# A two-layer encoder trunk on one core: two projection stages written out in program order with GpSimd reduced to one operation, and the attention buffers laid out anew around the last output weights

## The chip, the cores and the metric

The kernel runs on one core of one Trainium2 chip. The metric is the time of one execution in device microseconds (us), the median of several runs. A core has TensorE (PE; its weight loads are listed as PEld), VectorE (DVE), ScalarE (ACT), GpSimd (POOL) and SyncE (SP). DMAs are issued from SP and from ACT here, and both queues run on the same 16 DMA engines.

## The reference

Two layers of three parallel head groups over 1024 positions of width 1024, everything in float32:

```python
def hybrid_layer(x, g_norm, w_in, ...):
    h = rms_norm(x, g_norm)
    z = jnp.einsum('bsd,dc->bsc', h, w_in)             # 1024 -> 2656 columns
    aq, ak, av, ag, bq, bk, bv, bg, cq, ckv, ckr, cg = jnp.split(z, idx, axis=-1)
    qa, ka = (apply_axial_rope(rms_norm(t, g), ...) for t, g in ((aq, a_qn), (ak, a_kn)))
    oa = dense_gqa_blocks(qa, ka, va, HEAD_DIM ** -0.5) * jax.nn.silu(ag)      # A: 6 heads, 2 kv
    qb, kb = (apply_rope(t, ...) for t in (bq, bk))
    ob = windowed_sink_gqa(qb, kb, vb, b_sink, HEAD_DIM ** -0.5) * jax.nn.silu(bg)  # B: |i-j| <= 128
    qc = einsum(rms_norm(cq, c_qn), c_wuq); kv = einsum(rms_norm(ckv, c_kvn), c_wukv)
    oc = mla_blocks(qc_nope, rope(qc_rope), kc_nope, rope(ckr), vc, 96 ** -0.5) * jax.nn.silu(cg)  # C: 4 heads
    return x + jnp.einsum('bsm,md->bsd', concatenate([oa, ob, oc]), w_out)
```

A last RMSNorm closes the trunk.

## The kernel before

**Numbers.** Every float32 operand of a matmul is split into a rounded part (hi, the letter h at a tile's end) and a rest (lo, l); a product is three matmuls (`mm3`, L119). hi is a copy or cast on ACT or POOL, lo a subtraction on DVE that follows it.

**Stages of a layer.** The 1024 positions are 8 row tiles of 128 (`st`). (1) The rows are normalised, transposed to `hTh`/`hTl`, and the v columns of A and B are projected (`v_rows`). (2) **Stage A**, a loop over `st`: 24 matmuls of 512 columns give the q and k columns (`pza`), ACT copies them (`za`) and squares them (`ta`), DVE sums the squares (`ssa`, `ms_a`), POOL raises to the power -1/2 (`rs_a`, L113), DVE scales, and the axial rotation is a product with the cosines (`ta`, POOL L364), four products with the sines (`ua`, DVE L372) and a sum (DVE L377). `qk_out` transposes a finished row on PE (`pqka`, L301), splits it and stores it; `flush(2)` calls it two rows later. (3) **Stage B**, the same without the norm; its cosine product is POOL L397. In rows of A the weights of B are loaded and split step by step (`w_steps`: hi on POOL L196, lo on DVE L197), in rows of B those of C's projection. (4) C's latent projections, and the gates (`pg`, SiLU on ACT, stored by ACT's queue to `d_gate`). (5) **Attention**: `units` lists score units. For each `qt` (128 queries) and each of two kv heads there are three units of A and one of B; the scores are `sa`, `sb`, `sc`, the transposed probabilities `ppa`.. and the values `poa`... Behind the units of `2 * qt + kv` in `C_AT` comes a list of C's units. (6) **Output projection**: `out_part(st, c, ...)` sums 8 products with `Wo` into a bank of PSUM (`pw`), in two column halves c; the first `MW` = 5 of the 8 Wo tiles are used as spare work in the attention's end (`load_wo(wa_.wa, m)`), the last 3 come from a pool `wb` opened after it. DVE adds the residual (`y`, L1155), and the next layer's norm is mixed in.

**What sets the order.** A Tile scheduler reorders each engine's instructions by a simulated timeline, and pools decide which tiles share memory: a tile that lies over an older one waits for its last reader. SP issues its DMAs in one order; each carries one of eight semaphores (DMAHW0 to 7), taken in turn by the DMAs of SP and ACT, and waits there for the DMA that had it before.

**Memory in the attention.** The pools `at`, `ck` (k1, k2, k3 and the values `vC` of C), `qg` (C's queries `qc` and the gates gta, gtb, gtc) are stacked; `wb` opens over their upper part, on vC, qc and the gates. Stage (6) has three banks of PSUM for `pw` (`ps_s`); a fourth bank, `ps_o`, belongs to the value products.

Of the kernel before, what the change touches and what calls it, by code (L numbers as in the profile page):

```python
# [32 lines left out]
C_AT = (1, 3, 4, 6, 8, 9, 11, 13)  # L33
WARM = 12
PV_PRIO = 0
# [9 lines left out]
def kernel(  # L45
# [54 lines left out]

    ident = const.tile([P, P], F32, name="ident")
# [22 lines left out]
    class Stage:  # L124
# [17 lines left out]
        def norm(self, st, xt, src, junk):  # L142

            ss = small.tile([P, 1], F32, tag="ss1", name=f"ss{self.l}_{st}")
            nc.scalar.activation(junk, src, AF.Square, accum_out=ss)
            r = rstd_of(ss, D, f"x{self.l}_{st}", 1)
            nc.vector.scalar_tensor_tensor(xt, src, r[:, 0:1], self.ng, ALU.mult, ALU.mult)

        def turn(self, st, xt, ps_t):
            hf, c0 = st // 4, (st % 4) * P  # L150
            for g in range(2):
                pt = ps_t(f"pt{self.l}_{st}_{g}")
                for j in range(4):
                    nc.tensor.transpose(
# [14 lines left out]
        def w_steps(self, ws, pieces, eng=nc.vector, pool=None):  # L169
# [4 lines left out]
            for k0 in range(0, ND, kt):  # L174
# [31 lines left out]
    for l in range(DEPTH):  # L206
# [18 lines left out]
        with stage.ph as ph:  # L225
# [26 lines left out]
            def v_rows(st):  # L252
                ps = gemm_sc(stage.wv, st, f"pzv{l}_{st}")
                pv_ = ps[:, 0:256].rearrange("p (h d) -> p h d", d=64)
                nc.scalar.copy(vAB[:, st, :, 0:64], pv_)
                nc.vector.tensor_sub(vAB[:, st, :, 64:128], pv_, vAB[:, st, :, 0:64].bitcast(F32))

            if l == 0:
                stage.open_px()
                warm = ps_o("warm")  # L260
                for _ in range(WARM):
                    nc.tensor.matmul(warm[:, 0:P], lhsT=ident, rhs=ident, start=True, stop=True)
                xts = []
                for st in range(NS):
                    xts.append(stage.px.tile([P, D], F32, tag="xt", name=f"xt{l}_{st}", bufs=NS))
                    queue_behind[0] = dma(xts[st], x_src[st * P : (st + 1) * P, :])
                    if st == 0:
                        dma(stage.ng, norm_g[l].partition_broadcast(P))
                        stage.load_wv()
                for st, xt in enumerate(xts):  # L270
# [19 lines left out]
            dma(rope_b, c_rope_b.rearrange("(n p) t d -> p n t d", p=P))  # L290
            dma(rope_c, c_rope_c.rearrange("(n p) t d -> p n t d", p=P))
# [3 lines left out]
            def qk_out(u, g, st, nk):  # L295

                nm = f"{g}{l}_{st}"
                n = 3 + nk
                pt = ps_t(f"pqk{nm}")
                for j in range(n):  # L300
                    nc.tensor.transpose(pt[:, j * P : (j + 1) * P], u[:, j * P : (j + 1) * P], ident)  # L301
# [3 lines left out]
                nc.scalar.copy(hi[:, 0:n, :], ptv)  # L305
                nc.vector.tensor_sub(lo[:, 0:n, :], ptv, hi[:, 0:n, :].bitcast(F32))
# [945 lines left out]
```

## Time and profile before

| | |
|---|---|
| runs | 1353.19, 1356.27, 1358.64 us; median 1356.27 |
| the profiled execution | 1353.11 us, its span 1351.3 us, mean granted TensorE clock 0.993 |
| busy share of the span | PE 97%, PEld 84%, DVE 66%, ACT 52%, POOL 44% |
| DMA | 166.46 MB, mean 123 GB/s |

All times of a stage are counted in us from the span's start. In layer 0, stage A's matmuls begin at 44.2 and those of C's projection at 144.6, the gates end at 282.8, the attention runs to 588.8 and the output projection follows; the other layer repeats it some 670 us later. A PE busy share of 97% hides where its idle time lies, so a stage is read by windows and by waits.

### The profile page before, as it was taken

The page shows a single profiled execution, that of the slowest core. Times are in us where ns is not written, and L with a number is a line of the kernel's source. Part 1 is how long each engine was busy: PE and PEld are TensorE (multiplying, and loading weights), DVE is VectorE, ACT ScalarE, POOL GpSimd, SP SyncE. Part 2 cuts the span into 40 slices and gives each one's busy share as a digit, 9 for nine tenths or more (in the row PEclk, how much of TensorE's full clock was granted, in tenths as well). Part 3 has the DMA queues.
Part 4 walks back from the last instruction along what each step waited for, and adds up shares of the span by engine and source line. Part 5 has one row for each costly group of instructions (what it writes and reads, how often), then busy time and mean ns, then how long its engine had stood idle before and what let it go on. Part 6 is the DMA issues. An engine that isn't in the chain of part 4 may idle for free.

```text
span 1351.3 us, 21770 instructions
## 1 busy us (share of the span) xinstructions
PE 1307.1 (97%) x7320; PEld 1135.8 (84%) x7320; DVE 898.1 (66%) x2198; ACT 697.9 (52%) x1503; POOL 598.0 (44%) x694
## 2 busy tenths in 40 slices
PE   7999999999999999989999999999999999999897
PEld 7877998879998998867898779888799989988686
DVE  7586762058888889855436766610798889888533
ACT  5121341168888888712222214411788889887222
POOL 2564221026766766741025621200377676678200
PEclk9999999999999999999999999999999999999999
DMA  7333469443222511456323425694422225114443
GB/s 238 117 109 117 142 209 259 136 133 100 61 71 68 140 46 45 134 166 194 110 81 100 131 94 161 214 251 117 144 79 63 71 68 140 46 32 154 136 140 114
DMA packets 176879, 166.46 MB, mean 123 GB/s; under 512 B 22528, under 2 KB 149376, under 8 KB 176768
## 3 DMA queue, kind: packets, MB, share of 16 engines
q1 hardware_dynamic: 158016, 140.43, 35.6%
q10 hardware_dynamic: 18752, 24.65, 5.4%
q8 instruction: 58, 0.95, 0.3%
q14 instruction: 53, 0.43, 0.1%
HBM read 107.35 MB, written 57.67 MB: 122 GB/s over the span
## 4 chain that ended last, share of the span: by engine, by line
PE 64%; DVE 10%; ACT 6%; DMA 6%; POOL 5%; issue 4%; SPq 1%; POOLq 0%; DVEq 0%; ACTq 0%
PE pg L119 13%; PE pw L119 8%; PE poa L119 6%; PE ppa L655 5%; PE sa L119 4%; PE sc L119 4%; PE pzc L119 4%; PE pzb L119 4%; PE poc L119 3%; PE ppc L655 3%; DMA wst<-in_w_in_dram 2%; DVE ua L372 2%; PE pob L119 2%; PE sb L119 2%; POOL rs_a L113 2%
## 5 line engine op out<-in xcount | busy, mean ns | idle before, releaser
L636 DVE CUSTOM_DVE_ANT_0 pa<-sa,zero 128x512 f32<-128x512 f32 x96 | 65.6, 683 | 140.8 <-PE sa L119 135.1
L664 POOL TENSOR_TENSOR ptla<-pfa,ptha 128x512 fp32r<-128x512 f32 x96 | 123.9, 1293 | 5.8
L663 POOL TENSOR_SCALAR ptha<-pfa 128x512 fp32r<-128x512 f32 x96 | 59.7, 624 | 145.0 <-ACT pfa L662 136.7
L119 PE MATMUL sa<-ka,qsta 128*128 128x512 f32 x384 | 120.7, 417 | 0.7 <-ACT g L571 0.7
L646 ACT ACTIVATE pa<-pa,nmxa 128x1024 f32<-128x1024 f32 x96 | 111.3, 1161 | 17.7 <-DVE nmxa L636 15.6
L119 PE MATMUL pw<-woh,oh 128*128 128x512 f32 x256 | 101.1, 403 | 13.6 <-POOL woh L969 9.1
L119 PE MATMUL sc<-k,qc 128*128 128x512 f32 x384 | 109.9, 408 | 0.0
L655 PE MATMUL ppa<-ident,pa 128*128 128x128 f32 x768 | 107.3, 273 | 0.2
L655 PEld LDWEIGHTS ppa<-ident,pa 128*128 128x128 f32 x768 | 91.0, 141 | 14.2 <-DVE ptla L667 1.7
L119 PE MATMUL pw<-wol,oh 128*128 128x512 f32 x256 | 102.0, 400 | 0.4
L119 PE MATMUL pg<-hTh,wh 128*128 128x512 f32 x256 | 100.3, 392 | 0.0
L119 PE MATMUL pw<-woh,ol 128*128 128x512 f32 x256 | 99.9, 398 | 0.2 <-DVE ol L954 0.2
L119 PE MATMUL pg<-hTh,wl 128*128 128x512 f32 x256 | 100.1, 391 | 0.0
L119 PE MATMUL pg<-hTl,wh 128*128 128x512 f32 x256 | 100.0, 391 | 0.0
L196 POOL TENSOR_SCALAR wh<-wst 128x512 fp32r<-128x512 f32 (+2 forms) x96 | 59.2, 635 | 83.3 <-DMA wst<-in_w_in_dram 48.4
L119 PE MATMUL poa<-ptha,vAB 128*128 128x384 f32 x256 | 88.6, 346 | 0.9 <-ACT pc L646 0.5
L571 ACT ACTIVATE g<-pg 128x512 f32<-128x512 f32 x32 | 19.2, 599 | 134.8 <-PE pg L119 99.4
L119 PE MATMUL poa<-ptla,vAB 128*128 128x384 f32 x256 | 87.6, 342 | 0.0
L197 DVE TENSOR_TENSOR wl<-wst,wh 128x512 fp32r<-128x512 f32 (+2 forms) x96 | 67.5, 733 | 27.2 <-POOL wh L196 27.2
L646 ACT ACTIVATE pc<-pc,nmxc 128x1024 f32<-128x1024 f32 x64 | 74.2, 1161 | 10.0 <-DVE nmxc L636 9.5
L664 POOL TENSOR_TENSOR ptlc<-pfc,pthc 128x512 fp32r<-128x512 f32 x56 | 75.7, 1360 | 1.2
L119 PEld LDWEIGHTS sc<-k,qc 128*128 128x128 f32 x384 | 66.7, 189 | 9.9 <-DVE nmxc L636 0.9
(210 smaller groups left out, 3855.0 us busy)
## 6 DMA issues: line engine op xcount, KB each, us to landing
wst<-in_w_in_dram SPq DMA_DIRECT2D x20, 512.0 KB, 3.8
d_gate<-g ACTq DMA_DIRECT2D x32, 256.0 KB, 3.1
wost<-in_w_out_dram SPq DMA_DIRECT2D x32, 256.0 KB, 2.8
wst<-in_w_in_dram SPq DMA_DIRECT2D x16, 384.0 KB, 4.0
qsta<-d_qa SPq DMA_DIRECT2D x64, 96.0 KB, 2.8
qstb<-d_qb SPq DMA_DIRECT2D x64, 96.0 KB, 2.6
k<-d_kn SPq DMA_DIRECT2D x12, 512.0 KB, 5.8
qc<-d_qc SPq DMA_DIRECT2D x96, 64.0 KB, 2.2
```

Source lines behind the costliest of these rows:

```text
L113: last_pow[0] = nc.gpsimd.tensor_tensor(out=r, in0=ms, in1=mhalf[:, 0:w], op=ALU.pow).ins
L119: nc.tensor.matmul(ps, lhsT=a, rhs=b, start=first and i == 0, stop=last and i == len(parts) - 1)
L196: nc.gpsimd.tensor_scalar(h, f, 1.0, 0.0, ALU.mult, ALU.add)
L197: eng.tensor_tensor(out=r, in0=f, in1=h.bitcast(F32), op=ALU.subtract)
L372: nc.vector.tensor_mul(u5[:, h0:h1, :, a, :], z5[:, h0:h1, :, 1 - a, :], s5[:, :, a, :].unsqueeze(1).to_broadcast([P, nh, 2, 16]),)
L571: nc.scalar.activation(g, ps, AF.Silu)
L636: nc.vector.tensor_tensor_reduce(p[:, c * 512 : (c + 1) * 512], ps, zero[:, 0:1].to_broadcast([P, 512]), -1.0, nmx[0][:, 0:1] if c else 3. ...
L646: nc.scalar.activation(p, p, AF.Exp, scale=-1.0, bias=nmx[1][:, 0:1], accum_out=sm)
L655: nc.tensor.transpose(pt[:, (j - q0) * P : (j - q0 + 1) * P], p[:, j * P : (j + 1) * P], ident)
L663: nc.gpsimd.tensor_scalar(hi, f, 1.0, 0.0, ALU.mult, ALU.add)
L664: nc.gpsimd.tensor_tensor(out=lo, in0=f, in1=hi.bitcast(F32), op=ALU.subtract)
```

## The change

1. **Program order in A and B.** The engines are wrapped; while `pinned[0]` is set, an instruction keeps its place in program order. The two loops are written as a pipeline: a row's matmuls, the transposes of the row two before, ACT's square ahead of its copy, DVE's sums, POOL's power, the last sum of the row before (`add_halves`), the split of the transposed row (`qk_split`), one weight step, then the scaling and the products.
2. **GpSimd.** In A and B it keeps only the power; the cosine products go to DVE, the hi casts of B's and C's weights to ACT.
3. **Loads.** A's weights are asked for ahead of the tables, two rope tables after them; x has 6 buffers instead of 8.
4. **Pools of the attention.** New order `at`, `cv` (vC), `qg` (gates), `ck` (k1, k2, k3), `qc` (C's queries); `wb` opens over C's keys and queries.
5. **Output projection.** hi of the last three Wo tiles is made by ACT; one bank in four of `pw` is `ps_o`, and a fourth partial sum, (1, 1), joins the spare work.
6. **`C_AT`** starts (2, 3, 5, 6, ...) instead of (1, 3, 4, 6, ...).

```diff
-C_AT = (1, 3, 4, 6, 8, 9, 11, 13)
+C_AT = (2, 3, 5, 6, 8, 9, 11, 13)
+XBUFS = 6
+    pinned = [False]
+    class Engine:
+        def __init__(self, eng):
+            self.eng = eng
+        def __getattr__(self, op):
+            f = getattr(self.eng, op)
+            if not pinned[0]:
+                return f
+            return lambda *a, **k: tc.keep_in_program_order(f(*a, **k))
+    V, G, A, T = Engine(nc.vector), Engine(nc.gpsimd), Engine(nc.scalar), Engine(nc.tensor)
...
-                    nc.gpsimd.tensor_scalar(h, f, 1.0, 0.0, ALU.mult, ALU.add)
-                    eng.tensor_tensor(out=r, in0=f, in1=h.bitcast(F32), op=ALU.subtract)
+                    if hi_eng is A:
+                        A.copy(h, f)
+                    else:
+                        G.tensor_scalar(h, f, 1.0, 0.0, ALU.mult, ALU.add)
+                    V.tensor_tensor(out=r, in0=f, in1=h.bitcast(F32), op=ALU.subtract)
...
+            def add_halves():
+                for u, t in halves:
+                    V.tensor_add(u, t, u)
+                halves.clear()
+            pinned[0] = True
+            pb = pb_.enter_context(tc.tile_pool(name=f"pb{l}", bufs=1, reuse_waits="tile"))
+            ws_b = [], [], 512
+            steps = stage.w_steps(ws_b, [(1024, 512)], A, pb)
             for st in range(NS):
                 ps = gemm_sc(ws, st, f"pza{nm}")
-                flush(2)
+                old = late.pop(0) if len(late) > 1 else None
+                pt = qk_turn(*old) if old else None
-                nc.scalar.copy(z, ps)
                 nc.scalar.activation(t, ps, AF.Square, scale=0.125)
+                A.copy(z, ps)
...
+                add_halves()
+                if old:
+                    qk_split(pt, *old[1:])
+                if st:
+                    next(steps, None)
...
-                    nc.gpsimd.tensor_tensor(
-                        out=tv[:, h0:h1, :],
+                    V.tensor_mul(
+                        tv[:, h0:h1, :],
...
-                nc.vector.tensor_add(u, t, u)
+                halves.append((u, t))
...
-            ck = ph.enter_context(tc.tile_pool(name=f"ck{l}", bufs=1, reuse_waits="tile"))
+            cv = ph.enter_context(tc.tile_pool(name=f"cv{l}", bufs=1, reuse_waits="tile"))
             qg = ph.enter_context(tc.tile_pool(name=f"qg{l}", bufs=4, reuse_waits="tile"))
+            ck = ph.enter_context(tc.tile_pool(name=f"ck{l}", bufs=1, reuse_waits="tile"))
+            qc = ph.enter_context(tc.tile_pool(name=f"qc{l}", bufs=1, reuse_waits="tile"))
...
-                    wa_.ps[st, c] = ps_s(f"pw{l}_{st}_{c}")
+                    wa_.ps[st, c] = (ps_o if (2 * st + c) % 4 == 3 else ps_s)(f"pw{l}_{st}_{c}")
...
-            pipeline(units(), itertools.chain(*(out_part(*sc, 0, MW) for sc in ((0, 0), (0, 1), (1, 0)))))
+            pipeline(units(), itertools.chain(*(out_part(*sc, 0, MW) for sc in ((0, 0), (0, 1), (1, 0), (1, 1)))))
...
-                load_wo(wb, m)
+                load_wo(wb, m, A)
```

**In the order of the instructions, first: stage A of layer 0.** On POOL before, the power of a row stands between the cosine products and the weight casts (tile names end in the row and a running number):

```order
38 L113 TENSOR_TENSOR rs_a_3_806<-ms_a_3_804,mhalf 128x8
39 L364 TENSOR_TENSOR ta_3_798<-za_3_797,tabs_556 128x384
40 L364 TENSOR_TENSOR ta_3_798<-za_3_797,tabs_556 128x128
41 L113 TENSOR_TENSOR rs_a_4_871<-ms_a_4_869,mhalf 128x8
42 L364 TENSOR_TENSOR ta_4_863<-za_4_862,tabs_556 128x384
43 L364 TENSOR_TENSOR ta_4_863<-za_4_862,tabs_556 128x128
44 L113 TENSOR_TENSOR rs_a_5_928<-ms_a_5_926,mhalf 128x8
45 L364 TENSOR_TENSOR ta_5_920<-za_5_919,tabs_556 128x384
46 L364 TENSOR_TENSOR ta_5_920<-za_5_919,tabs_556 128x128
47 L196 TENSOR_SCALAR wh_11_1100<-wst_11_1099 128x352 x2
```

Now POOL has nothing but the eight powers there, and the products stand on DVE, whose row 3 reads (every row of A is L114 there, the wrapper's line):

```order
78 L114 TENSOR_REDUCE ssa_3_798<-ta_3_794 128x8
79 L114 TENSOR_SCALAR ms_a_3_800<-ssa_3_798 128x8
80 L114 TENSOR_TENSOR ua_2_730<-ta_2_729,ua_2_730 128x512
81 L114 TENSOR_TENSOR qkla_1_806<-pqka_1_788,qkha_1_805 128x512
82 L114 TENSOR_TENSOR wl_9_815<-wst_9_813,wh_9_814 128x512 x2
83 L114 TENSOR_TENSOR za_3_793<-za_3_793,rs_a_3_802 128x512
84 L114 TENSOR_TENSOR ta_3_794<-za_3_793,tabs_586 128x384
85 L114 TENSOR_TENSOR ua_3_795<-za_3_793,tabs_586 128x12x16 x2
86 L114 TENSOR_TENSOR ta_3_794<-za_3_793,tabs_586 128x128
87 L114 TENSOR_TENSOR ua_3_795<-za_3_793,tabs_586 128x4x16 x2
```

The row has twelve instructions; the sum of row 2 and the split of row 1 stand between the mean square and the scaling, which waits for the power.

**Second: SP at the start of the attention of layer 0.** Before, C's keys and values come first, then one of four loads of A's queries of `qt` = 1, then 15 loads of C's first queries:

```order
122 L96 DMA k_0_0_2808<-d_kn_83 64x2x1024 [waits DMAHW0_49,PE_49]
123 L96 DMA k_0_0_2808<-d_kn_83 64x2x1024 [waits DMAHW1_49]
124 L96 DMA k_0_2806<-d_kn_83 64x2x1024 [waits DMAHW3_49]
125 L96 DMA k_0_2806<-d_k_84 64x1024 [waits DMAHW4_49]
126 L96 DMA k_0_2806<-d_k_84 64x1024 [waits DMAHW5_49]
127 L96 DMA k_0_2807<-d_k_84 64x1024 [waits DMAHW6_49]
128 L96 DMA vC_0_2809<-d_vc_85 128x8x256 [waits DMAHW7_49]
129 L96 DMA qsta_1_3254<-d_qa_78 64x3x128 [waits DMAHW0_49,DVE_49,PE_49]
130 L96 DMA qc_0_0_2818<-d_qc_80 64x2x128 [waits DMAHW1_49]
131 L96 DMA qc_0_0_2818<-d_qc_80 64x2x128 [waits DMAHW2_49]
```

Now C's values and the gates are loaded first, and the keys stand behind A's queries of `qt` = 1 and the first of four loads of B's (`qstb_1`):

```order
129 L97 DMA qsta_1_3133<-d_qa_78 64x3x128 [waits DMAHW0_49]
130 L97 DMA qstb_1_3140<-d_qb_79 64x3x128 [waits DMAHW1_49]
131 L97 DMA k_0_0_2814<-d_kn_83 64x2x1024 [waits DMAHW2_49,Activation_49]
132 L97 DMA k_0_0_2814<-d_kn_83 64x2x1024 [waits DMAHW3_49]
133 L97 DMA k_0_2812<-d_kn_83 64x2x1024 [waits DMAHW4_49]
134 L97 DMA k_0_2812<-d_k_84 64x1024 [waits DMAHW5_49]
135 L97 DMA k_0_2812<-d_k_84 64x1024 [waits DMAHW6_49]
136 L97 DMA k_0_2813<-d_k_84 64x1024 [waits DMAHW7_49]
137 L97 DMA qc_0_0_2824<-d_qc_80 64x2x128 [waits DMAHW0_49]
138 L97 DMA qc_0_0_2824<-d_qc_80 64x2x128 [waits DMAHW1_49]
```

The other three loads of `qstb_1` stand behind the 15 loads of C's queries (the last nine of them):

```order
143 L97 DMA qc_0_1_2830<-d_qc_80 64x2x128 [waits DMAHW6_49]
144 L97 DMA qc_0_1_2830<-d_qc_80 32x2x128 [waits DMAHW7_49]
145 L97 DMA qc_0_1_2830<-d_qc_80 64x2x128 [waits DMAHW0_49]
146 L97 DMA qc_0_1_2830<-d_qc_80 32x2x128 [waits DMAHW1_49]
147 L97 DMA qc_0_2_2836<-d_qc_80 64x2x128 [waits DMAHW2_49]
148 L97 DMA qc_0_2_2836<-d_qc_80 64x2x128 [waits DMAHW3_49]
149 L97 DMA qc_0_2_2836<-d_qc_80 32x2x128 [waits DMAHW4_49]
150 L97 DMA qc_0_2_2836<-d_qc_80 64x2x128 [waits DMAHW5_49]
151 L97 DMA qc_0_2_2836<-d_qc_80 32x2x128 [waits DMAHW6_49]
152 L97 DMA qstb_1_3140<-d_qb_79 64x3x128 [waits DMAHW7_49]
153 L97 DMA qstb_1_3140<-d_qb_79 64x3x128 [waits DMAHW0_49]
154 L97 DMA qstb_1_3140<-d_qb_79 64x3x128 [waits DMAHW1_49]
```

On PE, where the first C scores stood before, A's units of `qt` = 1 stand now, and the first B scores of `qt` = 1 follow 36 instructions later (8 score matmuls of A, 24 transposes, 4 value matmuls of B). C's k1 lies over the buffers of the gates' results. The layer behind has the same order.

**Third: the last Wo tiles.** Before, POOL casts them behind the last gate product of C (`oc_1_6`):

```order
310 L719 TENSOR_TENSOR gtc_1_6_7048<-gtc_1_6_7048,rbc_1_6_7255 128x256
311 L1039 TENSOR_TENSOR oc_1_6_7046<-oc_1_6_7046,gtc_1_6_7048 128x256
312 L969 TENSOR_SCALAR woh_5_7345<-wost_5_0_7347 128x512
313 L969 TENSOR_SCALAR woh_5_7345<-wost_5_1_7351 128x512
314 L969 TENSOR_SCALAR woh_6_7355<-wost_6_0_7357 128x512
315 L969 TENSOR_SCALAR woh_6_7355<-wost_6_1_7361 128x512
316 L969 TENSOR_SCALAR woh_7_7365<-wost_7_0_7367 128x512
```

Now ACT casts them among the last probability casts (`pthc`) and the copies of the last value products (`ohc`):

```order
608 L714 CAST pthc_1_6_1_0_0_7193<-ppc_1_6_1_1_0_7236 128x4x128
609 L1018 CAST woh_5_7369<-wost_5_0_7371 128x512
610 L714 CAST pthc_1_6_1_0_1_7194<-ppc_1_6_1_1_4_7245 128x4x128
611 L1018 CAST woh_5_7369<-wost_5_1_7375 128x512
612 L765 COPY rbc_1_6_7261<-prc_1_6_7254 128x256
613 L1018 CAST woh_6_7379<-wost_6_0_7381 128x512
614 L1018 CAST woh_6_7379<-wost_6_1_7385 128x512
615 L736 COPY ohc_1_6_0_1_7287<-poc_1_6_0_1_7220 64x256
616 L1018 CAST woh_7_7389<-wost_7_0_7391 128x512
```

So the casts no longer stand behind C's last product, and PE has nine products with tiles 5 and 6 ahead of the last value product.

## Rows read from the trace of the kernel before

**Rows 1.** Windows of 25 us: length, busy us and instructions by engine, clock, DMA.

```profile
100.00:125.00 25.00, 21.89 (x97) 17.89 (x96) 19.75 (x30) 3.33 (x6) 12.94 (x12) 0.93 0.41 130
575.00:600.00 25.00, 20.68 (x103) 15.79 (x102) 13.46 (x19) 3.35 (x7) 10.92 (x16) 0.95 0.41 131
600.00:625.00 25.00, 21.22 (x84) 15.76 (x83) 16.00 (x22) 5.86 (x10) 7.18 (x10) 0.91 0.76 226
750.00:775.00 25.00, 22.57 (x101) 18.34 (x100) 19.39 (x37) 5.38 (x10) 17.73 (x20) 0.93 0.46 143
1250.00:1275.00 25.00, 19.88 (x96) 14.94 (x95) 12.91 (x19) 3.49 (x9) 7.51 (x10) 1.00 0.37 121
```

**Rows 2.** Waits of PE in 40 to 160 and 720 to 830: us, times, longest.

```profile
PE pqka L301 <- DVE ua L377: 5.2, 3, 3.1
PE pqka L301 <- DVE ua L377: 4.3, 2, 2.4
```

**Rows 3.** Window behind the stall at 113, PE alone: length, busy, clock, DMA.

```profile
113.00:116.00 3.00, 2.85 (x9) 0.50 0.23 76
```

**Rows 4.** Timeline of DVE in stage A: start, us, instruction, count, idle before.

```profile
75.68 1.29 DVE L377 TENSOR_TENSOR ua<-ta,ua 128x512 f32<-128x512 f32 x2
76.89 0.68 DVE L306 TENSOR_TENSOR qkla<-pqka,qkha 128x512 fp32r<-128x512 f32 x1
77.89 0.69 DVE L361 TENSOR_TENSOR za<-za,rs_a 128x512 f32<-128x512 f32 x1 [0.32 <-POOL rs_a L113]
78.62 1.99 DVE L372 TENSOR_TENSOR ua<-za,tabs 128x192 f32<-128x192 f32 x4
80.53 0.67 DVE L355 TENSOR_REDUCE ssa<-ta 128x8 f32<-128x512 f32 x1
```

**Rows 5.** Timeline of POOL in the same stretch.

```profile
75.85 2.01 POOL L113 TENSOR_TENSOR rs_a<-ms_a,mhalf 128x8 f32<-128x8 f32 x1 [0.65 <-DVE ms_a L111]
78.73 1.66 POOL L364 TENSOR_TENSOR ta<-za,tabs 128x384 f32<-128x384 f32 x2 [0.87 <-DVE za L361]
```

**Rows 6.** Groups of ACT's instructions in 44 to 125: count, busy, mean ns.

```profile
L305 ACT CAST qkha<-pqka 128x512 fp32r<-128x512 f32 x8 | 4.7, 590 | 2.5 <-PE pqka L301 2.4
```

**Rows 7.** Waits of PE in 575 to 625, and (last row) 1245 to 1275.

```profile
PE pw L119 <- POOL woh L969: 4.2, 3, 2.4
PE pw L119 <- DVE y L1155: 2.6, 1, 2.6
PE pw L119 <- POOL woh L969: 4.9, 3, 2.4
```

**Rows 8.** Timeline of PE at the first C scores.

```profile
294.92 0.86 PE L119 MATMUL sc<-k,qc 128*128 128x512 f32 x3
295.62 1.04 PE L655 MATMUL ppa<-ident,pa 128*128 128x128 f32 x8
296.41 0.94 PE L119 MATMUL sc<-k,qc 128*128 128x512 f32 x3
```

**Rows 9.** Timelines of ACT's and SP's queues (ACTq, SPq) at the attention's start.

```profile
283.67 0.33 ACTq L96 DMA_DIRECT2D d_gate<-g  x1
282.26 14.69 SPq L96 DMA_DIRECT2D qc<-d_qc  x15
300.42 2.56 SPq L96 DMA_DIRECT2D qstb<-d_qb  x4
```

**Rows 10.** Waits of SP in 248 to 306.

```profile
SPq L96 <- DMA d_gate<-g: 31.3, 6, 7.2
```

**Rows 11.** DMA issues, 248 to 306, last row 216 to 218.2: KB, us to landing.

```profile
d_gate<-g ACTq DMA_DIRECT2D x7, 256.0 KB, 2.4
k<-d_kn SPq DMA_DIRECT2D x3, 512.0 KB, 5.0
qstb<-d_qb SPq DMA_DIRECT2D x4, 96.0 KB, 2.6
ka<-d_ka SPq DMA_DIRECT2D x4, 512.0 KB, 8.0
```

More of the change, by code (lines that the diff above doesn't have):

```diff
@@ L118, in mm3 @@
         for i, (a, b) in enumerate(parts):
-            nc.tensor.matmul(ps, lhsT=a, rhs=b, start=first and i == 0, stop=last and i == len(parts) - 1)
+            T.matmul(ps, lhsT=a, rhs=b, start=first and i == 0, stop=last and i == len(parts) - 1)
     x_next = [dram.tile([S, D], F32, name=f"x_{l}") for l in range(DEPTH - 1)]
@@ L261, with load_x @@
                 for _ in range(WARM):
-                    nc.tensor.matmul(warm[:, 0:P], lhsT=ident, rhs=ident, start=True, stop=True)
-                xts = []
-                for st in range(NS):
[L265 to L270, printed above, removed]
+                    T.matmul(warm[:, 0:P], lhsT=ident, rhs=ident, start=True, stop=True)
+                xts = {}
+                def load_x(st):
+                    xts[st] = stage.px.tile([P, D], F32, tag="xt", name=f"xt{l}_{st}", bufs=XBUFS)
+                    queue_behind[0] = dma(xts[st], x_src[st * P : (st + 1) * P, :])
+                load_x(0)
+                dma(stage.ng, norm_g[l].partition_broadcast(P))
+                stage.load_wv()
+                for st in range(1, XBUFS):
+                    load_x(st)
+                for st in range(NS):
+                    xt = xts[st]
                     junk = stage.px.tile([P, D], F32, tag="junk", name=f"jk{l}_{st}", bufs=1)
@@ L295, in qk_out, with qk_turn, qk_split @@
             def qk_out(u, g, st, nk):
+                qk_split(qk_turn(u, g, st, nk), g, st, nk)
+            def qk_turn(u, g, st, nk):
+                pt = ps_t(f"pqk{g}{l}_{st}")
+                for j in range(3 + nk):
+                    T.transpose(pt[:, j * P : (j + 1) * P], u[:, j * P : (j + 1) * P], ident)
+                return pt
+            def qk_split(pt, g, st, nk):
                 nm = f"{g}{l}_{st}"
                 n = 3 + nk
-                pt = ps_t(f"pqk{nm}")
-                for j in range(n):
-                    nc.tensor.transpose(pt[:, j * P : (j + 1) * P], u[:, j * P : (j + 1) * P], ident)
                 hi = wk.tile([P, 4, P], F32R, tag="qkh", name=f"qkh{nm}")
@@ L714, in divided @@
                     ms = slice(m * P, (m + 1) * P)
[L715 removed]
+                    T.transpose(pr[:, ms], wide[:, ms], ident)
                 rb = at.tile([P, 384], F32, tag="rb", name=f"rb{nm}")
[L717 removed]
+                A.copy(rb[:, 0 : n * P], pr[:, 0 : n * P])
                 gv = gt.rearrange("p g s -> p (g s)") if len(gt.shape) == 3 else gt
[L719 removed]
+                G.tensor_tensor(out=gv, in0=gv, in1=rb[:, 0 : n * P], op=ALU.mult)
             class Gqa:
```

221 lines of the change are left out of this document (109 added, 112 removed).

## The prediction

> **What bounds the kernel now.** PE is busy for 97% of the span, so the end moves only where PE waits or runs at the lower of its two clock levels. I read the windows of 25 us first, looking for those in which PE is busy for less than 25 us or the clock is below 1.00. They lie at two places of each layer [rows 1]: stages A and B (21.89 us and clock 0.93 in 100 to 125, 22.57 and 0.93 in 750 to 775) and the output projection (20.68 and 0.95, then 21.22 and 0.91; 19.88 in the other layer). The waits of PE say what ends them: in A and B the transposes wait for the last sum of a row on DVE, 5.2 us in 3 waits and 4.3 in 2 [rows 2]; in the projection `pw` waits for the Wo casts on POOL, 4.2 and 4.9, and once for the residual addition that frees a bank, 2.6 [rows 7]. Behind a long stall the clock falls from 2.4 to 1.2 GHz: after the 3.1 us wait that ended at 113, three us ran at 0.50 [rows 3], which costs 1.5. The attention is read last, because there the change moves loads and not work.
>
> **A and B.** What it can give back is the waits and the clock: layer 0 5.2 + 0.07 x 25 = 7.0, layer 1 4.3 + 1.75 = 6.0 [rows 1, 2].
>
> Does DVE now keep up? PE needs 0.23 us for a matmul of 512 columns and 0.10 for a transpose, from the starts of neighbours [rows 8], so a row of 24 and 4 takes 5.9. On DVE, start to start, an operation of 512 elements takes 0.60 (two sums from 75.68 to 76.89), the scaling 0.73 (77.89 to 78.62) [rows 4]. The four sine products took 1.91 beside POOL's cosine products (78.62 to 80.53) [rows 4, 5]; by their 512 elements alone they would take 0.60, and I take 1.0. The cosine products, new on DVE, have 512 elements in two instructions: 0.65. A row of A with a weight step is then reduction 0.6, mean square 0.1, sum 0.6, split 0.6, two weight rests 1.2, scaling 0.7, cosines 0.65, sines 1.0: 5.45 us, and 4.25 without the step. With the sines at their contended 1.91 it is 6.35, but only in four rows of eight. A row's sum is wanted two rows later, so 0.45 in four rows (1.8) lies behind PE's work. If that cover were gone it would cost those 1.8 per layer. DVE's scaling waits for the power, 2.01 us [rows 5]; the sum, split and rests (2.4) stand in that wait.
>
> ACT takes two weight casts in eight rows of sixteen, 0.6 each like its others [rows 6]; it was busy for only 3.33 of 25 us in 100 to 125 [rows 1], so I cost them at nothing; with its cover gone, four rows would pay 1.2 each. What pinning may cost is at A's first row: PE may no longer take later rows while A's last weights are split. I allow 0.5 per layer. Sum for A and B: -13 + 1 = -12; bounds -14 and, with both covers gone, -5.
>
> The Trainium skill, page "SBUF — State Buffer", section "SBUF: two separate sides", says that VectorE and GpSimd share a port pair as an exclusive lock: an operation with two SBUF inputs and a GpSimd operation that reads SBUF block each other for a whole instruction. Beside the cosine products the trace agrees (1.91 against 0.60 by elements); beside the power it doesn't: in the 2.01 us from 75.85 the second sum of 512 elements ran its usual 0.60 [rows 4, 5]. By the rule a row with a weight step would be 5.45 + 2.0 = 7.5; by the rows it stays 5.45. I go by the rows.
>
> **The output projection.** Tiles 5 to 7 lie over memory that the last C scores release, ahead of the last value product, and their casts no longer stand behind the last gate product. The waits for them end: 4.2 and 4.9 [rows 7]. The fourth bank ends the wait of 2.6. The clock was lost at 0.05 x 25 + 0.09 x 25 = 3.5 in layer 0 [rows 1]; with no stall over 2 us it stays up. Layer 0: 4.2 + 2.6 + 3.5 = 10.3 and two shorter waits, 11.5; layer 1: 4.9 and the slow restart behind three waits, 5.5. Against that: ACT's casts stand ahead of a probability cast and of a copy that frees the value bank. Nine products with tiles 5 and 6 (2.1 us) and the rest of row 1 are there for PE meanwhile; without this cover the wait for the last value product is as long as the one removed, and half the saving goes. Sum -17, bounds -8 and -19.
>
> **The attention's start.** Here I expect a new wait. B's first scores of `qt` = 1 need the four loads `qstb_1`; three stand behind six loads of C's keys and 15 of its queries.
> - When do the keys go out? k1 lies over the gates' buffers, so it waits for the last store of a gate, issued at 283.67 [rows 9] and landing 2.4 later [rows 11]: 286.1. SP waited 31.3 us for such stores before as well, six times [rows 10]; then its keys had the length of the gates for it.
> - How long do they take? One load of 512 KB landed 5.0 after its issue; of four issued together the median was 8.0 [rows 11], so one follows another by about 3.0 / 1.5 + 0.65 = 2.65. Three of 512 KB and three of half that size: 286.1 + 5.0 + 2 x 2.65 + 3 x 1.3 = 300.3 for the last.
> - What queues behind? The 8th query load takes the semaphore of the last key load (DMAHW7 in both), so it and the seven behind it go out after 300.3, 0.64 each (four in 2.56) [rows 9]: the missing `qstb_1` go out at 305.4 to 306.7 and land 2.6 later [rows 11], 308.0 to 309.3.
> - When does PE want them? It is at the place of the first C scores at 294.92 [rows 8]; 8 score matmuls, 24 transposes and 4 value matmuls are 1.9 + 2.4 + 0.7 = 5.0: 299.9.
>
> PE waits 8.1 for the first and some 0.4 more for the others: 8.5, and 1.5 at the lower clock [rows 3]. That is 10 per layer and 20 in all. Bounds: were the keys' landing to cost nothing, the 24 issues of 0.64 from 286.1 still bring the last of `qstb_1` to 286.1 + 23 x 0.64 + 2.6 = 303.4, a wait of 3.5; were the keys to land one by one (5.0 each, half size by half), 286.1 + 22.5 + 6.4 + 2.6 = 317.6, 17.7. The same in layer 1, where every piece has the same place. C's own keys, now wanted later, are landed by then.
>
> **Sum.** -12 - 17 + 20 = -9 against the profiled 1353.11: 1344. That execution lies 3.2 below the median of the runs, whose spread is 5.5; I don't add it in full: **1344**.
>
> **The rivals.** A difference under 0.5%, 6.8 us, can't be told from none here.
> 1. *The loads come in time.* If the stores land early and the keys overlap better than `ka` did, the wait is 3.5 per layer with no loss of clock: -29 + 7 = -22, 1331; with all of A's and the projection's gains 1327, and 1324 if SP's issues are quicker too. For it: `ka` did overlap, and a store lands in 2.4 [rows 11]. Against it: SP alone needed 14.69 us for 15 query loads [rows 9]. The Trainium skill, "DMA: Bandwidth & Descriptors", section "Issuing engines are not separate DMA queues", calls the time of an issue usually small beside the DMA itself; these 15 show 0.64 and more each.
> 2. *DVE becomes the bound of A.* If the power holds DVE for its 2.0, four rows per layer take 7.5 and four 6.25 against 5.9: 4 x 1.6 + 4 x 0.35 = 7.8 per layer, of which I let the two rows between a sum and its transposes take half: 4 lost per layer. Of the 12 then 4 are left: 1353 - 17 + 20 - 4 = 1352. Against it: the sum beside the power [rows 4, 5]. The rule of the Trainium skill quoted above is this case.
> 3. *ACT's casts hold up the last value product.* Then the projection gives 8 and not 17: 1353.
> 4. *Slower.* The keys land one by one: SP sends each only when the one before has landed, as they did before, when each waited for a gate's store. Then the wait is 17.7 + 1.5 = 19 per layer, 38 in all: 1353 - 29 + 38 = 1362, and by the median 1365. It decides above 14.5 per layer. Against it: `ka`, four in a row, overlapped [rows 11].
>
> That the order isn't changed can be excluded: the rows of the order show it.
>
> **How the numbers follow.** Forecast 0.50 (1337 to 1351), first rival 0.22, second and third 0.17, fourth 0.11. Most of the forecast (0.40) and the first rival, and 0.04 of the others, are over 6.8 below the median: faster 0.66, same 0.24, slower 0.10. The range leaves out the fourth rival and the best of the first: 1325 to 1356.
>
> **What the profile will show.** No wait of PE on `ua` or its successor in A and B, POOL with powers only, clock 1.00 there; `pw` without waits for casts or banks; one wait of PE for `qstb_1` near 300 and 970, ended by a DMA, and a clock of 0.5 behind it. Wrong it is if that wait is missing (I then misread the lanes or the stores), if A's transposes still wait for DVE, or if DVE's sums stretch beside the power.

## The result, and the profile after

The changed kernel takes 1341.86 us (median of four runs, 1340.09 to 1342.25); the kernel before, timed beside it, takes 1355.03. The ratio is 0.9897, 95% interval 0.9873 to 0.9921: faster by about 1%, 13 us. The forecast was 1344, the range 1325 to 1356. Beside the sets of runs below the kernel before took 1353.09 to 1354.06, so times of different sets compare to some 2 us. The profiled execution has a span of 1340.4, against 1351.3.

The windows of the changed kernel (length, then busy us and instructions of PE, PEld, DVE, ACT and POOL, the clock, DMA share and GB/s); five of them answer to [rows 1]:

```profile
0.00:25.00 25.00, 17.77 (x93) 16.20 (x94) 14.81 (x25) 13.67 (x25) 7.36 (x14) 0.87 0.81 266
100.00:125.00 25.00, 25.00 (x120) 20.69 (x119) 15.51 (x30) 8.07 (x17) 0.00 (x0) 1.00 0.52 159
275.00:300.00 25.00, 21.03 (x115) 16.18 (x113) 19.24 (x61) 20.24 (x45) 9.99 (x11) 0.97 0.69 159
300.00:325.00 25.00, 21.31 (x115) 19.12 (x116) 16.45 (x44) 15.02 (x35) 9.60 (x11) 0.83 0.34 93
575.00:600.00 25.00, 24.50 (x136) 20.47 (x136) 18.83 (x31) 11.78 (x23) 13.93 (x15) 1.00 0.49 170
600.00:625.00 25.00, 25.00 (x119) 20.55 (x118) 15.60 (x22) 5.75 (x10) 7.40 (x10) 1.00 0.83 248
750.00:775.00 25.00, 25.00 (x121) 20.76 (x120) 16.14 (x35) 8.48 (x17) 1.94 (x1) 1.00 0.44 134
950.00:975.00 25.00, 18.50 (x97) 15.98 (x96) 17.36 (x46) 15.60 (x39) 9.84 (x12) 0.80 0.44 113
1250.00:1275.00 25.00, 22.27 (x100) 16.95 (x99) 10.95 (x22) 8.74 (x19) 1.98 (x3) 1.00 0.46 150
```

Stage A and the output projection of layer 0, which had 21 to 22 busy us of 25, are full or nearly so and at clock 1.00. The holes have moved to 275 to 325 and to 950 to 975, the start of the attention, and the second layer's output projection keeps a part of its own. The waits of PE in the whole span (us in all, times, longest) name the new one first; of the others on the list these are the output projection's longest:

```profile
PE sb L136 <- DMA qstb<-d_qb: 12.8, 4, 6.5
...
PE pw L136 <- ACT oh L1001: 1.1, 1, 1.1
...
PE pw L136 <- ACT woh L1018: 1.0, 2, 0.6
```

No wait of a transpose (`pqka`, `pqkb`) is on the list. The wait of 12.8 us is B's first scores of `qt` = 1 in both layers, 6.7 and 6.1. SP's timeline around it, and PE's (start, us, instruction, in brackets the idle time before and what ended it):

```profile
280.02 0.65 SPq L97 DMA_DIRECT2D qstb<-d_qb  x1
281.90 2.19 SPq L97 DMA_DIRECT2D k<-d_kn  x3
284.15 1.87 SPq L97 DMA_DIRECT2D k<-d_k  x3
286.06 14.86 SPq L97 DMA_DIRECT2D qc<-d_qc  x15
300.97 1.82 SPq L97 DMA_DIRECT2D qstb<-d_qb  x3
```

```profile
296.50 0.44 PE L703 MATMUL ppb<-ident,scb 128*128 128x128 f32 x2 [0.35 <-ACT pfa L710]
303.45 0.98 PE L136 MATMUL sb<-kb,qstb 128*128 128x384 f32 x2 [6.50 <-DMA qstb<-d_qb]
```

Three of four loads of `qstb_1` go out behind 15 query loads, at 300.97, and PE stands from 296.95 to 303.45. The stretch behind the stall runs at the lower clock in both layers (windows of PE alone: length, busy, clock, DMA):

```profile
303.20:312.00 8.80, 8.31 (x33) 0.69 0.62 170
960.50:968.00 7.50, 6.90 (x23) 0.54 0.63 180
```

That is an estimated 8.8 x 0.31 = 2.7 and 7.5 x 0.46 = 3.5 us more.

The stages' lengths, from the first matmul of one to that of the next (`pza`, `pzc`, `sa`, the next layer's `pza`, the end; differences of starts rounded to 0.1), show where the time went:

| stage | before | after | moved | forecast |
|---|---|---|---|---|
| start to A, layer 0 | 44.2 | 47.2 | +3.0 | 0 |
| A and B, layer 0 | 100.4 | 93.5 | -6.9 | -6.5 |
| C's projection and gates, layer 0 | 138.2 | 138.0 | -0.2 | 0 |
| attention, output projection, start of layer 1 | 428.3 | 425.2 | -3.1 | +10 - 11.5 |
| A and B, layer 1 | 101.0 | 93.6 | -7.4 | -5.5 |
| C's projection and gates, layer 1 | 140.3 | 139.1 | -1.2 | 0 |
| attention and output projection, layer 1 | 398.9 | 403.8 | +4.9 | +10 - 5.5 |
| span | 1351.3 | 1340.4 | -10.9 | -9 |

The second layer's attention and output projection are slower than before the change; A and B carry the result.

### The profile page after: what moved, and what is told of

The parts are those of the page before. It is cut to its first block, busy times and chain, and to the rows that moved or that the text cites. A ratio compares the mean times of both kernels' runs of the same rounds, so it can differ in the third digit from the quotient of the medians.

```text
span 1340.4 us, 21695 instructions
## 1 busy us (share of the span) xinstructions
PE 1301.9 (97%) x7320; PEld 1139.5 (85%) x7320; DVE 892.3 (67%) x2246; ACT 720.2 (54%) x1547; POOL 524.6 (39%) x602
## 4 chain that ended last, share of the span: by engine, by line
PE 82%; DVE 6%; DMA 5%; ACT 2%; issue 2%; SPq 2%; POOL 1%; POOLq 0%; DVEq 0%; ACTq 0%
PE pg L136 13%; PE pw L136 12%; PE pzb L114 7%; PE pza L114 7%; PE poa L136 6%; PE sc L136 5%; PE ppa L703 4%; PE pzc L136 4%; PE sa L136 4%; PE pzv L136 4%; PE ppc L703 3%; PE poc L136 3%; PE pob L136 2%; PE sb L136 2%; SPq L97 2%
## 5 line engine op out<-in xcount | busy, mean ns | idle before, releaser
L216 POOL TENSOR_SCALAR wh<-wst 128x512 fp32r<-128x512 f32 (+1 forms) x64 | 39.6, 638 | 148.3 <-PE pzb L114 79.4
L684 DVE CUSTOM_DVE_ANT_0 pa<-sa,zero,nmxa 128x512 f32<-128x512 f32 x96 | 71.1, 743 | 4.5 <-PE sa L136 1.8
```

The source lines that it names most:

```text
L216: G.tensor_scalar(h, f, 1.0, 0.0, ALU.mult, ALU.add)
L684: V.tensor_tensor_reduce(p[:, c * 512 : (c + 1) * 512], ps, zero[:, 0:1].to_broadcast([P, 512]), -1.0, nmx[0][:, 0:1] if c else 3.0e38, AL ...
```

## The experiments

**The attention's start: e1.** The theory is that the wait is SP's order and nothing else. The edit loads the four `qsta_1` and all four `qstb_1` ahead of C's keys, and touches loads alone. The scheduler then also reorders the engines, but only from the place where B's scores can start sooner: up to 295.8 PE has the same instructions in both kernels.

```diff
+                    if hp == 0:
+                        dma(self.v, d_vc[:, :, 0:2, :])
+                        start["a"].gate()
+                        start["b"].gate()
+                        start["second"] = Gqa("a", 1, 0), Gqa("b", 1, 3)
                     for r0 in (0, 64):
                         dma(self.k1[r0 : r0 + 64], ...)
...
-                        a, b = Gqa("a", qt, 0), Gqa("b", qt, 3)
+                        a, b = start["second"] if qt == 1 else (Gqa("a", qt, 0), Gqa("b", qt, 3))
```

> The changed kernel with SP's order at the attention's start altered: C's values and two gates, then all eight loads of the queries of qt = 1 for A and B, then C's keys, then C's queries. Theory (B's loads stood behind C's): PE's wait for qstb, 6.7 and 6.1 us, and the low clock behind it are gone, some 10 us per layer; C's queries come some 2 us later and cost 1 to 4 per layer again: 1328 us, 1322 to 1335. Rival (the DMA engines are full of C's keys, whatever is asked for first): the wait moves to C's first scores with the same length, 1338 to 1343.

Measured: 1340.12 us (1338.71 to 1343.96), ratio to before 0.9907 (0.9886 to 0.9929). The wait is gone. The windows 275 to 325 and 950 to 1000, PE alone, first of the changed kernel, then of e1:

```profile
275.00:325.00 50.00, 42.35 (x230) 0.90 0.51 126
950.00:1000.00 50.00, 43.50 (x255) 0.90 0.35 93
```

```profile
275.00:325.00 50.00, 48.46 (x284) 1.00 0.55 140
950.00:1000.00 50.00, 48.81 (x296) 1.00 0.50 124
```

So the cause is SP's order. Yet the median fell by only 1.7 us, less than the spread of the runs. By the traces the attention and projection became 4.2 us shorter in layer 1 and 5.7 longer in layer 0, where the planned order of SP's loads changed at the other end too. Waits of PE in e1's 560 to 640, and SP's timeline there:

```profile
PE pw L136 <- ACT oh L1001: 9.5, 2, 7.4
```

```profile
602.98 10.28 SPq L97 DMA_DIRECT2D wst<-in_w_in_dram  x6
613.36 1.00 SPq L97 DMA_DIRECT2D ol<-d_o  x2
```

Six loads of the next layer's weights, two of which wait for buffers that DVE frees, now stand ahead of the rows (`ol`) that the output projection needs: a queue was blocked behind a waiting load a second time.

**The rows ahead of the weights: e5.** e1's edit, and the next layer's first weight loads behind the last row loads:

```diff
+            if l:
+                queue_behind[0] = last_ol[0]
             ws = load_w([(0, 512)])
...
-                dma(lo, d_o[:, m0:m1, st * P : (st + 1) * P])
+                last_ol[0] = dma(lo, d_o[:, m0:m1, st * P : (st + 1) * P])
```

> The kernel with the queries of A and B asked for first at the attention's start, and besides the second layer's loads of A's weights ordered on SP behind the last load of attention results in the first layer's output projection. Theory (the attention's start is worth 15 us and was eaten by a new wait of 7.4 us for attention results that stood on SP behind weight loads which wait for DVE): that wait and the low clock behind it go, 10 us off the kernel before it: 1330 us, 1326 to 1334. Rival (the results are late for another reason, their own stores): the wait stays, 1338 to 1342.

Measured: 1335.26 us (1333.45 to 1337.91), ratio 0.9864 (0.9844 to 0.9885), 6.6 less than the changed kernel. Waits in 560 to 640:

```profile
PE pw L137 <- ACT oh L1004: 4.9, 2, 3.1
```

Half of e1's wait has gone, the attention's start stays full. The median misses the 1326 to 1334 expected by 1.3.

**The rest of that wait: e11 and e12.** e11 is e5 with the broadcast of the next layer's norm weights (`ng`, 128 x 1024) issued behind two row loads; e12 adds `WV_ST = 3`, which is to split the next layer's value weights one row later.

```diff
+                out_rows(6, 8, 1)
+                queue_behind[0] = last_ol[0]
                 dma(stage.ng, norm_g[l + 1].partition_broadcast(P))
+                queue_behind[0] = wo_ins[0]
```

> The version with A's and B's second queries loaded ahead of C's keys and the row loads of the output projection ahead of the next layer's weights (1335.3 measured, 1331.8 profiled), and with the broadcast of the next layer's norm weights (ng, 128 x 1024) put behind the two row loads ol_2_0 and ol_1_6 on SP instead of ahead of them. If those two landed late (591.79 and 592.16, 3 to 6 us after their issue) because the 512 KB of ng moved ahead of them, PE's first wait for oh, 1.8 us, goes and the clock stays up: 1332 to 1334. If they were late because they are issued behind the last store of oc, the wait stays, and so does the time, 1335.

> The kernel of the run above with the next layer's value weights (W_V, four rests of 1.1 us on DVE) split one row later in the output projection of layer 0 (WV_ST 3 instead of 2). If PE's second wait there (3.1 us for oh at 610 to 614) comes from those rests, which stood ahead of y of row 1 on DVE while ACT's cast of the row (oh) stood behind the norm of y, it goes: 2 to 4 us faster than the run above. If the rests hold up a row whenever they come, the wait moves to the next row and the time stays within 1 us of the run above.

Measured: e11 1333.04 us (1331.47 to 1335.13), ratio 0.9841 (0.982 to 0.9862); e12 1332.33 (1329.87 to 1334.41), 0.9834 (0.9812 to 0.9856). In e11, 2.2 us below e5 and within the spread of both, one of e5's two waits is gone:

```profile
PE pw L137 <- ACT oh L1004: 3.9, 1, 3.9
```

e12 can't answer its question: DVE's timeline has the four rests ahead of `y` as in e11, so the edit didn't move them.

```profile
605.41 3.76 DVE L218 TENSOR_TENSOR wl<-wst,wh 128x512 fp32r<-128x512 f32 x4 [7.58 <-POOL wh L217]
```

What the last 4 us wait hangs on stays untested. The trace of e11 shows this chain: the rows have landed by 607.09; ACT casts the row (`oh`, 610.52) right behind its square of `y`, for which it sat idle for 7.0 us until 609.46; on DVE that `y` (608.75) stands behind the four rests (603.28 to 607.03), and DVE was idle for 6.7 before them, waiting for POOL's casts. e11 and e12 are the fastest kernels of the study, equal within their intervals.

**C_AT alone: e10.** The changed kernel with `C_AT = (1, 3, 4, 6, ...)`.

> The changed kernel with C_AT starting (1, 3, 4, 6) as before. C's first scores then stand at the place of A's of qt = 1, which PE reaches near 286. If SP's queue is what binds there, they wait for the keys k2 and k3 (landed 292.6 to 296.2 in the changed kernel's trace) for some 5 to 8 us from the place where PE comes to them, and B's scores of qt = 1, some 45 instructions later (8 us), then find qstb_1 landed or nearly so (303.3 to 305.0): the wait changes its name from qstb to k and stays 5 to 8 us per layer, 1338 to 1345 in all. If the move of C_AT itself saved time, the waits for k and for qstb add up to 10 us or more per layer: 1348 or more. If C_AT's move was what made the new wait, PE waits under 2 us: 1330 or less.

Measured: 1343.04 us (1340.67 to 1343.9), ratio 0.9912 (0.9895 to 0.9928). Waits of PE in 275 to 340, and its first row in 560 to 640:

```profile
PE sc L136 <- DMA qc<-d_qc: 2.8, 1, 2.8
...
PE pw L136 <- ACT oh L1001: 7.2, 2, 6.0
```

C's scores wait 2.8 us in each layer for their queries (not for the keys, as I had expected), and B's then find theirs: the move of `C_AT` more than doubled the wait at this place. Of the 6.4 us of wait, 2.8 belong to the new order of loads alone, the rest to that table. The total doesn't show it, since e10 has the same kind of wait for `oh` as e1, with the same order on SP: six weight loads from 602.44 on, then two row loads.

**Which part of the change freed A and B: e2, e3, e6, e7.** e2 only sets `pinned[0] = False`. e3 puts the cosine products back on POOL:

```diff
-                    V.tensor_mul(tv[:, h0:h1, :], zv[:, h0:h1, :], ...)
+                    G.tensor_tensor(out=tv[:, h0:h1, :], in0=zv[:, h0:h1, :], ..., op=ALU.mult)
```

e6 does both; e7 is e3 with the weight casts back on POOL too (`w_steps` without `A`).

> The changed kernel with the two loops of A and B left to the scheduler (nothing pinned); the work stays on the engines where the change put it. Theory one (the order is what counts): PE waits in A and B come back in part, 4 to 7 us per layer, 1349 to 1356 us. Theory two (moving the cosine products off GpSimd is what counts): no waits of PE there, 1340 to 1344.

> The changed kernel, pinned as it is, with the cosine products of A and B back on GpSimd. Theory one (the order counts): a sum is wanted two rows later, the sines stretch to 1.9 us beside the cosines and still fit, 1340 to 1344 us. Theory two (the engine counts): DVE's row goes beyond PE's 5.9 or the chain through GpSimd is late, 3 to 7 us per layer, 1348 to 1356.

> The changed kernel with A and B left to the scheduler and the cosine products back on GpSimd; of the change in A and B there remain the weight casts on ACT, the square ahead of the copy and the later sum. Theory (the casts on GpSimd held up the powers): no waits of PE in A and B, 1340 to 1344 us. Rival (one of order and products has to be changed): waits come back, 4 to 7 us per layer, 1349 to 1356.

> The changed kernel, pinned, with the cosine products and the weight casts of B and C back on GpSimd, so that GpSimd has in each row the power 2.0, products 1.7 and, in rows with a weight step, two casts of 0.6 to 0.7: 5.1 us. Theory (the casts on GpSimd held up the powers, whatever the order): waits come back, 1347 to 1355 us. Rival (the written order is enough): none, 1340 to 1344.

| | order written | products | casts | us | ratio to before (95%) |
|---|---|---|---|---|---|
| changed | yes | DVE | ACT | 1341.86 | 0.9897 (0.9873 to 0.9921) |
| e2 | no | DVE | ACT | 1340.59 | 0.9900 (0.9877 to 0.9923) |
| e3 | yes | POOL | ACT | 1343.14 | 0.9922 (0.9903 to 0.9941) |
| e6 | no | POOL | ACT | 1353.84 | 0.9998 (0.9989 to 1.0007) |
| e7 | yes | POOL | POOL | 1351.11 | 0.9983 (0.9971 to 0.9994) |

In e2 and e3 PE has no wait in A or B. In e6, then in e7 (40 to 170), the one of [rows 2] is back:

```profile
PE pqka L327 <- DVE ua L381: 3.6, 3, 2.4
PE pqka L327 <- DVE ms_a L128: 0.9, 2, 0.7
```

```profile
PE pqka L114 <- DVE ua L114: 4.1, 3, 1.8
```

Neither the written order nor the move of the products is needed by itself; with the casts on ACT either one does. The waits come back when POOL has other work around the power: the products in the scheduler's order, or products and casts, in the written order (e7) as in the scheduler's (the kernel before). Which step then makes PE wait isn't shown: POOL is later, but DVE is slower too. The groups of the larger sine products (instructions, busy us, mean ns) in 48 to 138, first of the changed kernel, then of e3, show what the products on POOL alone do to DVE:

```profile
L114 DVE TENSOR_TENSOR ua<-za,tabs 128x192 f32<-128x192 f32 x16 | 4.9, 351 | 0.0
```

```profile
L114 DVE TENSOR_TENSOR ua<-za,tabs 128x192 f32<-128x192 f32 x16 | 11.5, 762 | 0.3
```

In e3 that doubling costs nothing: PE has no wait there. A and B are worth 1353.84 - 1341.86 = 12.0 us, and 13.7 by the ratios. The traces agree: in e6 C's projection starts 5.6 us later in layer 0 and A and B take 6.9 longer in layer 1, 12.5 in all (at nearly the same clock in the first 25 us, 0.86 and 0.87). In layer 1 A and B take 101.0 before, 98.3 in e7, 100.4 in e6 and 93.5 in the changed kernel: the written order alone gives 2.7 of the 7.5 us, the casts on ACT alone 0.6, and the casts with either the order (e3) or the products on DVE (e2) the whole. The products on DVE with the casts left on POOL weren't tried.

**The output projection: e8 and e9.** e8 leaves the last Wo casts on POOL, `load_wo(wb, m)`, in the new memory layout. e9 has three banks again: `ps_s` alone and no fourth partial sum.

> The changed kernel with the last three output weights cast by GpSimd as before, and the new layout of memory kept. Theory (the memory they lay over was the wait): the casts run early all the same, 1341 to 1344 us. Rival (GpSimd's queue was the wait): the waits for woh come back, 4 to 5 us per layer, 1348 to 1352.

> The changed kernel with three banks for the output projection again: no partial sum lies in ps_o, and the fourth partial sum (1, 1) is no spare work of the attention's end. If the fourth bank is what ended the wait for the residual addition (2.6 us in layer 0 of the kernel before) and its 15 products are cover for the last value product, PE waits again in 575 to 625, for y and for the row's oh or woh, 3 to 6 us in the two layers together: 1345 to 1348. If the new memory layout alone gives the gain of the output projection, PE has no new wait there and the time is that of the changed kernel, 1340 to 1343.

Measured: e8 1346.86 us (1344.33 to 1349.33), ratio 0.9948 (0.9929 to 0.9968); e9 1345.72 (1344.37 to 1347.87), 0.9935 (0.9916 to 0.9954): 5.0 and 3.9 above the changed kernel. Waits of PE in e8, first row of 560 to 640, first two of 1220 to 1345:

```profile
PE pw L136 <- ACT oh L1001: 2.3, 1, 2.3
...
PE pw L136 <- DVE oc L1123: 3.6, 1, 3.6
PE pw L136 <- POOL woh L1020: 1.1, 1, 1.1
```

In layer 0 the 4.2 us for `woh` [rows 7] stay away even with POOL's casts: there the layout removed them. The row (`oh`) that PE waits for there comes late from SP, which issues its load at 614.04 behind two weight loads (it lands at 619.58, PE goes on at 620.13); so this part isn't shown to be the casts'. In layer 1 PE waits 4.9 us in all, against 3.0 in the changed kernel, and the clock is 0.93 in 1250 to 1275, against 1.00: there the move to ACT pays. In e9 (560 to 640) the bank's wait is back, and the clock drops behind it:

```profile
PE pw L136 <- DVE y L1206: 3.0, 1, 3.0
```

```profile
600.00:625.00 25.00, 22.02 (x97) 17.76 (x96) 15.84 (x22) 5.74 (x10) 7.53 (x10) 0.93 0.76 229
```

**x's buffers: e4.** `XBUFS = 8` as before, since the start of layer 0 had grown by 3 us.

> The changed kernel with eight buffers for the rows of x, as before. The first stage ends 3 us later with the change than before (first matmul of A at 47.2 instead of 44.2) and shows clocks of 0.66 and 0.69. Theory (the last rows of x come late): the 3 us come back, 1339 us. Rival (the loads of x have nothing to do with it; the clock fell for another reason): 1341 to 1343, with the first matmul of A still near 47.

Measured: 1347.77 us (1346.13 to 1351.62), ratio 0.9965 (0.9951 to 0.9979). The first `pza` starts at 44.1, but that isn't the buffers' doing. Ten kernels have 6 buffers and the same instructions on every engine up to the start of A (the changed one, e1, e3, e5, e7 to e12). A starts at 44.1 to 44.4 in six of them, with a clock of 1.00 in the first 25 us, at 45.5 in e8 (0.93), and at 47.2 to 47.5 in three (0.87 and 0.88). What sets that clock stays open. The first window of e9, to set beside the changed kernel's 0.87:

```profile
0.00:25.00 25.00, 17.10 (x116) 15.36 (x117) 16.05 (x30) 14.88 (x27) 6.93 (x16) 1.00 0.80 265
```

e4 is slower for another reason, PE's wait for `oh` in 560 to 640, 7.9 us in two waits. SP has the order of e1 there, six weight loads from 605.51 on and then two row loads; that this is the cause here too wasn't tried.

**The stages of all runs.** From the traces, in us: when A and C's projection start in layer 0, how long A and B take in layer 1, and how long the attention and the output projection take, in layer 0 to the next layer's A, in layer 1 to the end.

| | A starts | C's projection starts | A and B, layer 1 | attention on, layer 0 | attention on, layer 1 |
|---|---|---|---|---|---|
| before | 44.2 | 144.6 | 101.0 | 428.3 | 399.0 |
| changed | 47.2 | 140.7 | 93.5 | 425.3 | 403.8 |
| e1 | 47.2 | 140.7 | 93.5 | 431.0 | 399.6 |
| e2 | 42.8 | 139.0 | 93.5 | 428.9 | 402.4 |
| e3 | 44.1 | 137.7 | 93.5 | 427.0 | 403.6 |
| e4 | 44.1 | 137.7 | 93.5 | 435.8 | 401.3 |
| e5 | 44.1 | 137.6 | 93.5 | 426.6 | 396.9 |
| e6 | 44.3 | 146.3 | 100.4 | 427.9 | 401.8 |
| e7 | 44.4 | 142.7 | 98.3 | 428.0 | 403.1 |
| e8 | 45.5 | 139.0 | 93.5 | 430.1 | 405.9 |
| e9 | 44.3 | 137.8 | 93.5 | 431.4 | 403.4 |
| e10 | 44.1 | 137.7 | 93.5 | 433.0 | 399.9 |
| e11 | 44.2 | 137.7 | 93.5 | 423.8 | 398.3 |
| e12 | 47.5 | 141.0 | 93.5 | 424.0 | 397.0 |

Each row is one execution. The changed kernel, e2, e3, e6 and e7 have the same code from the attention on, and their lengths there differ by up to 3.6 us in layer 0 and 2.0 in layer 1; smaller differences in the last two columns say nothing. The sum of the two columns is steadier: 827.3 before, 829.1 to 831.3 in these five.

## Why the prediction was right

- **A and B, -12.** Right: PE's waits are gone, and the size is 12.0 by e6 against the changed kernel and 14.3 in the first table of the stages, a little over the outer bound of 14. (The inner bound, -5, isn't what its terms give: -12 + 3.6 + 4.8 = -3.6.) DVE does a row in 5.92 us (from one scaling's start at 73.97 to the next at 79.89), PE's pace, and its cosine and sine products cost what was estimated. DVE and then POOL in a row of A:

```profile
74.69 0.56 DVE L114 TENSOR_TENSOR ta<-za,tabs 128x384 f32<-128x384 f32 x1
75.17 0.62 DVE L114 TENSOR_TENSOR ua<-za,tabs 128x192 f32<-128x192 f32 x2
75.71 0.28 DVE L114 TENSOR_TENSOR ta<-za,tabs 128x128 f32<-128x128 f32 x1
75.91 0.35 DVE L114 TENSOR_TENSOR ua<-za,tabs 128x64 f32<-128x64 f32 x2
...
77.00 0.68 DVE L114 TENSOR_TENSOR ua<-ta,ua 128x512 f32<-128x512 f32 x1
77.61 0.68 DVE L114 TENSOR_TENSOR qkla<-pqka,qkha 128x512 fp32r<-128x512 f32 x1
78.67 1.29 DVE L114 TENSOR_TENSOR wl<-wst,wh 128x512 fp32r<-128x512 f32 x2 [0.39 <-ACT wh L114]
```

```profile
77.24 1.94 POOL L114 TENSOR_TENSOR rs_a<-ms_a,mhalf 128x8 f32<-128x8 f32 x1 [3.64 <-DVE ms_a L114]
```

  Start to start the sines take 0.54 + 0.29 = 0.83 (1.0 forecast, 1.91 before, beside POOL's products) and the cosines 0.48 + 0.20 = 0.68 (0.65). Rival 2 falls: DVE doesn't wait for the power. The sum keeps its 0.68 us, but it starts 0.24 ahead of the power; the better test is the weight rests (`wl`, two inputs in SBUF), of which the first here starts inside the power, at 78.67. In A of layer 0 six rests do, and each takes 0.68 to 0.69 us. By the rule of the Trainium skill, page "SBUF — State Buffer", section "SBUF: two separate sides", a power that has started would have held up such a rest to its end; this trace doesn't show it, as far as POOL's spans, which are rough, can tell, and the measurement decides. The 1 us allowed for pinning at A's first row didn't appear.
- **The output projection, -17.** Layer 0 was right: in 575 to 625 idle time and clock give 7.6 + 3.5 = 11.1 back [rows 1], 11.5 forecast. Layer 1 was oversized: in 1250 to 1275 PE gained 22.27 - 19.88 = 2.4 of the 5.5, because short waits for `oh`, `woh` and `wol` took the place of the long one. The clock stayed up in both layers, as forecast. The condition given for it, no stall over 2 us, isn't enough, though: in e9 it is 0.93 in 1250 to 1275, where no wait is longer than 0.9. ACT's casts held up no value product (rival 3).
- **The attention's start, +20.** The place, the load and the queue were as forecast. The keys took 14.3 us from the first issue to the last landing, 14.2 forecast; the eighth query load went out at 296.20, when the last key had landed (296.19), and the others and `qstb_1` followed. Where PE stands, the size is nearly right too: 6.7 + 2.7 and 6.1 + 3.5, 19.0 in all. Its two pieces were off in opposite ways: the wait 6.4 in the mean and not 8.5, the clock 3.1 and not 1.5, because the price of the clock came from a stall of 3 us. But not all of it lasts: A's last scores come 6.4 and 6.6 us later than in e1 (259.1 against 252.7 after the first, 259.2 against 252.6), so 13 of the 19 are left there, and the forecast carried 20 to the end. All times there were some 4 us earlier than I wrote (keys issued at 281.90, not 286.1), since I hadn't moved them up by what A and B had gained; PE's place moved with them, by 3. The keys overlapped, against rival 4 (one by one): all six landed between 286.92 and 296.19. Rival 1 failed by the keys, which landed no faster than forecast, and not by SP's issues. Of SP's 14.86 us for the 15 query loads 6.1 were waits for keys (SP's waits in 279 to 306):

```profile
SPq L97 <- DMA k<-d_kn: 4.0, 2, 2.4
SPq L97 <- DMA k<-d_k: 2.1, 3, 1.0
```

  The 14.69 us before [rows 9], which the prediction read as SP's own need, likewise hold 4.7 of waiting for a gate's store; most issues alone take 0.6 or less.
- **Start, 0.** The +3.0 wasn't foreseen, and isn't the change's: executions with the same instructions there show it or not (e4).
- **Sum.** The layer totals came out 1.6 better (layer 0) and 0.4 worse (layer 1) than forecast for attention and projection together, A and B 2.3 better, the gates 1.4 better. The median fell by 13.2, which is 2 more than the profiled spans say; the changed kernel's profiled execution had the late start. The forecast for attention and projection in sum was +3, the first table says +1.8, and the five kernels with this code give +1.8 to +4.0. The pieces named above don't add up as well: 19.0 - 11.1 - 2.4 = +5.5, or -0.5 with the 13 that last. So the mechanism of each term is shown, but that the total came within 2 us is partly luck: the price of the attention's start and the gain in layer 1's projection were both forecast too large, and they cancel.

## What to carry to other kernels

A queue that issues in one order turns a memory layout into a schedule: when loads move because their buffers now lie over something else, follow what is queued behind each waiting load, on the queue's whole length, since a repair at one end (e1) can open the same hole at the other. A change made of several parts can be redundant: with the casts on ACT, the written order and the move of the products each removed the same wait, and only undoing both showed its worth. When a gain is taken from one place and paid at another, price both; here 1333 us was to be had by the order of the loads alone.

## What the runs showed of the hardware

- The clock's price isn't read off the stall's length: behind waits of 6.5 and 5.6 us PE ran 7 to 9 us at a mean of 0.69 and 0.54, an estimated 2.7 and 3.5 us, so the shorter wait cost more; a stall of 3.1 had cost 1.5 [rows 3].
- The first 25 us run at a granted clock of 1.00 in some executions and of 0.87 in others with the same instructions, and stage A then begins 3 us later (47.2 against 44.3).
- The four sine products of 512 elements take 0.83 us with POOL idle and 1.91 beside POOL's cosine products [rows 4, 5]; e3, which differs from the changed kernel by those products alone, has the larger ones at 0.76 us each, against 0.35. POOL's power has no such effect on the weight rests (0.68 to 0.69 us).
- A load on SP whose semaphore is still in use waits for the load that had it before: the eighth query load was issued at 296.20, when the last key had landed at 296.19, and `qstb_1` stood behind it.
